# Ten of the twelve column blocks of the mixer's input projections as seven block products, their results kept in DRAM

## The chip, the core and the metric

One core of a Trainium2 chip. Five engines work side by side, each in its own program order: PE (matrix products; its weight loads are listed as PEld), DVE and ACT (element-wise work), POOL, and SP, which only issues transfers. They wait for each other through semaphores. Working memory is SBUF (128 partitions); matrix products land in PSUM, in banks of 128 x 512 fp32. The metric is the device time of one execution in microseconds.

## What is computed

One layer of a hybrid decoder for 512 tokens of width 2048, in fp32:

```python
def token_mixer(h, ...):
    proj = h @ w_in
    gq, gk, gv, gg, ga, dq, dk, dv = [...]
    log_a = jax.nn.log_sigmoid(ga @ w_alpha_up + b_alpha) / GLA_TAU
    o_a = gla_chunked(gq, gk, gv, log_a)
    o_a = rmsnorm(o_a, gla_norm) * jax.nn.silu(gg)
    o_b = rmsnorm(diff_attention(dq, dk, dv, lam), diff_norm) * (1.0 - lambda_init)
    return jnp.concatenate([o_a, o_b], axis=-1) @ w_o

x = x + rmsnorm(token_mixer(rmsnorm(x, attn_pre_norm), ...), attn_post_norm)
x = x + rmsnorm(conv_ffn(rmsnorm(x, ffn_pre_norm), ...), ffn_post_norm)
```

There are four heads of gated linear attention (GLA; queries and keys 128 wide, values 256) and four of differential attention (two pairs of queries and keys of 128, values 256). `conv_ffn` is a gated MLP of width 5632 with a short convolution; the change does not touch it.

## The kernel before

**Products.** Every fp32 operand is kept as a high and a low half, and a product is three matmuls: high by high, high by low, low by high. The normed tokens stand transposed in `ah` and `al`, 16 slices of 128 of the 2048 inputs. Weights come in granules of 512 KB (128 x 1024) into `raw` tiles, four of them; for each granule ACT copies the high half (L136) and DVE subtracts it for the low half (L137), both into `ring`, which has three slots for each half. A slot is free again when PE has used it.

**Column blocks.** The mixer's input weights are twelve blocks of 512 columns: GV (two), GQ with GK (256 columns each, two), DV (two), DQ with DK (four) and the gate GG (two). `proj_n` (L190 to L192) makes rows of tokens: tokens are the stationary operand, 512 weight columns move, eight granules of two slices. `proj_t` (L172 to L174) makes transposed results for queries and keys: 128 weight columns are stationary, 512 tokens move, four granules for 256 columns. Both take 192 matmuls of 512 columns for a block. Results stay in SBUF: `gv`, `dv`, the q and k tiles, `oa` (GLA's output, gated in place by `gate`) and `dst` (the differential heads' output, already transposed).

**Heads.** The forget gate (`forget_gate`, L396 to L408), the GLA heads and the differential heads are generators in a list `fill`. After each granule `step` moves the first one on, 1.7 steps per granule at first and 1.0 from the first differential head on. A differential head goes through four blocks of 128 queries. For each there are two score products (L508), the softmax (max, exponential, sums; L510 to L524, where L523 scales and L524 subtracts the second map from the first), the transposes (L531), the product with the values (L539) and the transposes of the result (L551). Within a block each step waits for the one before.

**What sets the order.** A scheduler puts each engine's instructions in order when the kernel is built; on the chip each engine follows that order. Only the first half of the first block and the passage to the FFN are written out by hand.

**The FFN's up projection** already has the form that the change brings to the mixer: with the tokens in two halves, the inputs in two and the columns in two, a product of 2 x 2 blocks is made from seven products in place of eight (class `Unit`, segments `x0`, `z0`, `y0`, `z1`, `x1`, `y1`, `y2`). The token sums for it are made once. The weight sums are made partly by DVE and partly by transfers that add to what lies in SBUF (`more`, issued by POOL). Its matmuls (L928 to L930) have 256 columns, and its halves lie in `ring` at the offsets `APART = (16, 112)`, while the mixer's are at `LEVEL = (0, 0)`.

Of the kernel before, what the change touches and what calls it, by code (L numbers as in the profile page):

```python
# [9 lines left out]
F32 = mybir.dt.float32  # L10
# [7 lines left out]
P = 128  # L18
# [17 lines left out]
def hybrid_layer(ctx: ExitStack, tc: tile.TileContext, x, attn_pre_norm, w_in, w_alpha_up, b_alpha,  # L36
# [69 lines left out]
    LEVEL, APART = (0, 0), (16, 112)  # L106
# [99 lines left out]
    mixer = ExitStack()  # L206
    mx1 = mixer.enter_context(tc.tile_pool(name="mx1", bufs=1))
    mx = mixer.enter_context(tc.tile_pool(name="mx", bufs=6))

    def big8(name):  # L210
        return mx.tile([P, 2048], F32, name=name, tag="big8", bufs=6)

    def qk_tile(name):
        return mx.tile([P, S], F32, name=name, tag="qk", bufs=6)

    def tmp(name, shape=(P, S)):
        return mx.tile(list(shape), F32, name=name, tag="tmp")


    def first_half(c):  # L220
        gb = big8("gb")
        jb = mx.tile([P, 1024], F32, name="jb", tag="jb", bufs=1)
        xts = [big8("xt") for _ in range(NT)]
        w3 = mx.tile([P, 2, GR], F32R, name="w3", tag="big8", bufs=6)
# [84 lines left out]
    gv = [big8("gv").rearrange("p (t e) -> p t e", t=NT) for _ in range(2)]  # L309

    def gv_out(c):
        return lambda t, b: act(gv[c][:, t, :], b, AF.Copy)

    proj_n(w_in3, C_GV, gv_out(0), first=4, banks=banks)


    dist = mx1.tile([P, S], F32, name="dist")
    nc.gpsimd.iota(dist, [[-1, S]], base=S - P, channel_multiplier=1, allow_small_or_imprecise_dtypes=True)
    nc.gpsimd.affine_select(dist, dist, [[-1, S]], ALU.is_ge, 1e34, base=S - P, channel_multiplier=1)
    masks = mx1.tile([P, 7, 4 * 64], U8, name="masks")  # L320
    setup = big8("setup")
    for li, hs in enumerate(LEVELS):
        nb = 64 // hs
        m = setup[:, 1024 + 64 * li:1024 + 64 * (li + 1)]
# [5 lines left out]
    keep = mx1.tile([P, S], F32, name="keep")  # L330
    nc.vector.memset(keep, 1.0)
    nc.vector.memset(keep.rearrange("p (c x) -> p c x", c=4)[:, :, 0:1], 0.0)
    gnb = mx1.tile([P, GDV], F32, name="gnb")
    bcast_row(gnb, gla_norm[0])
    dnb = mx1.tile([P, DDV], F32, name="dnb")
    bcast_row(dnb, diff_norm[0])
    ts(dnb, dnb, 1.0 - LAMBDA_INIT, None, ALU.mult)

    lam = few.tile([P, 1], F32, name="lam")
    lt = setup[:, 0:512].rearrange("p (a d) -> p a d", a=4)  # L340
    for i, v in enumerate((lambda_q1, lambda_k1, lambda_q2, lambda_k2)):
        bcast_row(lt[:, i, :], v[0])
    lp = setup[:, 512:768].rearrange("p (a d) -> p a d", a=2)
# [10 lines left out]
    rows = setup[:NF, 1536:2048].rearrange("p (a d) -> p a d", a=4)  # L354
    ba = setup[:4, 768:896]
# [12 lines left out]


    bcs = big8("bcum")  # L370
    bcum = [bcs[:, h * S:(h + 1) * S] for h in range(GH)]

    def forget_gate():
        gar = tmp("gar").rearrange("p (k r) -> p k r", r=RANK)[:, :KT, :]
        dma(gar, w_in3[:, :, C_GA:C_GA + RANK])
        gas = mx.tile([P, KT, 80], F32R, name="gas", tag="big8", bufs=6)
        nc.vector.memset(gas.bitcast(F32), 0.0)
        split(gas[:, :, 0:RANK], gas[:, :, 64:64 + RANK], gar)
        wup = mx.tile([80, GH * GDK], F32, name="wup", tag="tmp")
        nc.vector.memset(wup, 0.0)  # L380
        dma(wup[0:RANK, :], w_alpha_up[0])
        dma(wup[64:64 + RANK, :], w_alpha_up[0])
        yield
# [5 lines left out]
        gaT = mx.tile([80, S], F32, name="gaT", tag="tmp")  # L389
# [3 lines left out]
        a = big8("za")  # L393
        for h in range(GH):
            zb = bank()
            mm(zb, wup[:, h * P:(h + 1) * P], gaT, start=True, stop=True)  # L396
            bcol = cols[:, h:h + 1]
            act(a[:, h * S:(h + 1) * S], zb, AF.Abs, bias=bcol)
            ts(bcum[h], zb, bcol, 0.0, ALU.add, ALU.min)
            if h % 2:  # L400
                yield
# [946 lines left out]
```

## Time and profile before

| | us |
|---|---|
| median of three runs | 2148.33 |
| their range | 2145.24 to 2149.51 |
| the profiled execution | 2149.06 |
| its span | 2147.3 |
| of it: start, 0 to 68.09 | 68.09 |
| input blocks and heads, 68.09 to 640 | 571.91 |
| end of the last gate block, transposes, 640 to 665 | 25.00 |
| output projection, 665 to 797 | 132.00 |
| passage to the FFN, 797 to 934 | 137.00 |
| up projection, 934 to 1685 | 751.00 |
| down projection and end, 1685 to 2147 | 462 |

The granted clock of the core is 0.998 over the span. Over the whole span PE is busy 2109.6 us (98%), DVE 1414.1 (66%), ACT 897.5 (42%) and POOL 199.6 (9%); these shares are averages over stages with different limits. A matmul's busy time overlaps with the next one's, so PE's pace is read from the distance between starts.

### The profile page before, as it was taken

To read this page: it belongs to the slowest core of one execution; us is meant where nothing else is said; L and a number is where in the kernel's file an instruction comes from. 1 tells how busy PE (TensorE), PEld (TensorE's weight loads), DVE (VectorE), ACT (ScalarE), POOL (GpSimd) and SP (SyncE) were. 2 spreads that over 40 slices of the span, in tenths; PEclk is the share of its full clock that TensorE was granted. 3 is DMA by queue.
4 is the path that set the end of the run, shared out by engine and by line. 5 is a ranking of instruction groups with operands and counts; after the bars stand their busy time and mean duration, and the time that the engine had idled before them with its cause. 6 is when DMAs were issued, how large, how long until landed. Compare 5 with 4: busy or idle time off the path is not lost.

```text
span 2147.3 us, 31857 instructions
## 1 busy us (share of the span) xinstructions
PE 2109.6 (98%) x13009; PEld 1872.4 (87%) x13009; DVE 1414.1 (66%) x1725; ACT 897.5 (42%) x1162; POOL 199.6 (9%) x242
## 2 busy tenths in 40 slices
PE   7999999999999999999999999999999999999998
PEld 6878888888888888899999999999999877788786
DVE  5345554443444237588778777787877867888887
ACT  4233332333343224345444444554454654443433
POOL 1000000000000001010111101111011111110100
PEclk9999999999999999999999999999999999999999
DMA  6322222223224335356775767758577787676653
GB/s 214 100 74 79 79 70 79 79 79 85 78 84 167 98 128 186 118 116 145 167 182 133 165 166 170 170 131 198 144 168 194 201 227 178 171 196 171 164 163 144
DMA packets 218471, 303.83 MB, mean 141 GB/s; under 512 B 11776, under 2 KB 155572, under 8 KB 216404
## 3 DMA queue, kind: packets, MB, share of 16 engines
q1 hardware_dynamic: 165204, 238.87, 33.4%
q0 software_dynamic: 53120, 62.92, 18.9%
q8 instruction: 102, 1.67, 0.3%
q14 instruction: 45, 0.37, 0.1%
HBM read 273.97 MB, written 27.79 MB: 141 GB/s over the span
## 4 chain that ended last, share of the span: by engine, by line
issue 51%; PE 40%; POOL 4%; DVE 2%; DMA 2%; ACT 1%; POOLq 0%; SPq 0%; DVEq 0%; ACTq 0%
PE bank L190 7%; PE bank L191 7%; PE bank L192 7%; PE bank L174 5%; PE bank L172 5%; PE bank L173 5%; POOL rt L876 2%; POOL raw L876 2%; PE bank L440 1%; PE bank L508 1%; PE bank L539 1%; PE bank L157 1%; DMA raw<-in_w_ffn_out_dram 1%; DVE ring L137 1%; DMA xt<-in_x_dram 1%
## 5 line engine op out<-in xcount | busy, mean ns | idle before, releaser
L137 DVE TENSOR_TENSOR ring<-raw,ring 128x1024 fp32r<-128x1024 f32 x305 | 371.8, 1222 | 357.1 <-ACT ring L136 350.0
L136 ACT ACTIVATE ring<-raw 128x1024 fp32r<-128x1024 f32 x305 | 322.5, 1060 | 605.1 <-PE bank L192 157.3
L930 PE MATMUL bank<-ah,ring 128*128 128x256 f32 x1280 | 353.5, 276 | 0.8 <-DVE ring L137 0.8
L928 PE MATMUL bank<-ah,ring 128*128 128x256 f32 x1280 | 353.4, 276 | 0.0
L929 PE MATMUL bank<-al,ring 128*128 128x256 f32 x1280 | 353.3, 276 | 0.0
L137 DVE TENSOR_TENSOR ring<-rt,ring 128x1024 fp32r<-128x1024 f32 x221 | 269.0, 1221 | 91.4 <-ACT ring L136 91.0
L136 ACT ACTIVATE ring<-rt 128x1024 fp32r<-128x1024 f32 x221 | 233.1, 1059 | 226.6 <-PE bank L929 144.7
L930 PEld LDWEIGHTS bank<-ah,ring 128*128 128x128 f32 x1280 | 240.3, 188 | 1.0 <-DVE ring L137 1.0
L928 PEld LDWEIGHTS bank<-ah,ring 128*128 128x128 f32 x1280 | 240.3, 188 | 0.3 <-ACT ring L136 0.2
L929 PEld LDWEIGHTS bank<-al,ring 128*128 128x128 f32 x1280 | 240.3, 188 | 0.1
L190 PE MATMUL bank<-ring,ah 128*128 128x512 f32 x600 | 236.8, 398 | 0.4 <-ACT ah L149 0.4
L191 PE MATMUL bank<-ring,ah 128*128 128x512 f32 x600 | 235.6, 393 | 0.0
L192 PE MATMUL bank<-ring,al 128*128 128x512 f32 x600 | 234.9, 393 | 0.0
L172 PE MATMUL bank<-ah,ring 128*128 128x512 f32 (+1 forms) x512 | 195.8, 383 | 1.9 <-ACT ring L136 1.9
L174 PE MATMUL bank<-ah,ring 128*128 128x512 f32 (+1 forms) x512 | 194.2, 380 | 0.1
L173 PE MATMUL bank<-al,ring 128*128 128x512 f32 (+1 forms) x512 | 194.2, 379 | 0.0
L1031 PE MATMUL bank<-ring,ah 128*128 128x512 f32 x424 | 166.3, 392 | 4.7 <-DVE ring L137 4.7
L1032 PE MATMUL bank<-ring,al 128*128 128x512 f32 x424 | 165.2, 390 | 0.0
L1030 PE MATMUL bank<-ring,ah 128*128 128x512 f32 x424 | 158.4, 391 | 1.4 <-ACT ring L136 1.0
L192 PEld LDWEIGHTS bank<-ring,al 128*128 128x128 f32 x600 | 113.0, 188 | 24.2 <-DVE al L150 0.3
L191 PEld LDWEIGHTS bank<-ring,ah 128*128 128x128 f32 x600 | 113.3, 189 | 23.7 <-DVE ring L137 0.5
L190 PEld LDWEIGHTS bank<-ring,ah 128*128 128x128 f32 x600 | 113.1, 189 | 23.7 <-ACT ah L149 0.8
(263 smaller groups left out, 4062.8 us busy)
## 6 DMA issues: line engine op xcount, KB each, us to landing
raw<-in_w_in_dram SPq DMA_DIRECT2D x96, 512.0 KB, 3.7
raw<-in_w_ffn_in_dram SPq DMA_DIRECT2D x96, 512.0 KB, 5.2
raw<-in_w_ffn_out_dram SPq DMA_DIRECT2D x48, 512.0 KB, 6.5
rt<-in_w_ffn_in_dram SPq DMA_DIRECT2D x40, 512.0 KB, 5.7
rt<-in_w_ffn_in_dram POOLq DMA_DIRECT2D x40, 512.0 KB, 6.1
raw<-in_w_ffn_in_dram POOLq DMA_DIRECT2D x40, 512.0 KB, 7.1
raw<-in_w_o_dram SPq DMA_DIRECT2D x32, 512.0 KB, 3.7
rt<-in_w_ffn_out_dram SPq DMA_DIRECT2D x20, 512.0 KB, 8.2
```

The lines of the kernel that those rows point to most:

```text
L136: act(hi, raw, AF.Copy)
L137: tt(lo, raw, hi.bitcast(F32), ALU.subtract)
L172: mm(o, wh, ah[:, t0:t1, kk, :], start=st, stop=False)
L173: mm(o, wh, al[:, t0:t1, kk, :], start=False, stop=False)
L174: mm(o, wl, ah[:, t0:t1, kk, :], start=False, stop=sp)
L190: mm(banks[t], ah[:, t, s, :], w[0][:, k, :], start=st, stop=False)
L191: mm(banks[t], ah[:, t, s, :], w[1][:, k, :], start=False, stop=False)
L192: mm(banks[t], al[:, t, s, :], w[0][:, k, :], start=False, stop=sp)
L928: mm(o, wh, sh[:, :, kk, :], start=start and kk == 0 and n == 0, stop=False, **NOW)
L929: mm(o, wh, sl[:, :, kk, :], start=False, stop=False, **NOW)
L930: mm(o, wl, sh[:, :, kk, :], start=False, stop=kk == HK - 1, **NOW)
L1031: mm(b[j], sh[:, o:o + P], w[1][:, q, :], start=False, stop=False, **NOW)
```

## The change

Two of the twelve blocks stay: GV 0 by `proj_n`, and GQ and GK of heads 0 and 1 by `proj_t`. The ten others become units (`InUnit`) of seven segments. `rows_unit` (GV 1, both DV) and `gate_unit` (both GG) have the token sums as stationary and 256 weight columns as moving operand (L699 to L701 of the changed kernel; offsets `APART_N`, the two of `APART` exchanged). `pair_unit` (GQ with GK, DQ with DK) has weights stationary and 256 tokens moving (L695 to L697). The ring's slots get a stride of 1152 elements in place of 1024. `in_sums` makes the token sums s5, s2 and s3 in six tiles, and s7, which takes the place of a quarter of `ah` and `al`.

For room, results go to DRAM (`gvd`, `dvd`, `gqd`, `gkd`, `dqd`, `dkd`, `bcd`, `oad`, `dstd`, `ogd`), and each head loads what it needs into one value tile and four tiles for queries and keys. The forget gate works on four tiles, one for each head, in place of one. The scale of L523 goes from DVE to ACT, and the product of decay and key is made for the half that is used. `pace` is 1.35 at first and 0.62 in the units. At the end, `place_diff` loads and splits the differential heads' results, and `turn_gate` transposes the gated ones, around the last unit's segments.

```diff
-    LEVEL, APART = (0, 0), (16, 112)
+    LEVEL, APART, APART_N = (0, 0), (16, 112), (112, 16)
+    RS = GR + P
     place_w = [LEVEL]
...
-        return [ring[:, GR * i + p:GR * (i + 1) + p] for i, p in zip((slot[0], slot[0] + 3), place_w[0])]
+        return [ring[:, RS * i + p:RS * i + p + GR] for i, p in zip((slot[0], slot[0] + 3), place_w[0])]
...
+    def in_sums():
+        for i in range(2):
...
+            q = flat("q")
+            tt(q, a21[0], a22[0], ALU.subtract)
+            tt(q, q, a21[1], ALU.add)
+            tt(q, q, a22[1], ALU.subtract)
+            split(sums["s5"][0][:, i], sums["s5"][1][:, i], q)
...
+            s7raw.append(r)
+            yield
...
-        a = big8("za")
+        za, bt = [], []
         for h in range(GH):
             zb = bank()
             mm(zb, wup[:, h * P:(h + 1) * P], gaT, start=True, stop=True)
             bcol = cols[:, h:h + 1]
-            act(a[:, h * S:(h + 1) * S], zb, AF.Abs, bias=bcol)
-            ts(bcum[h], zb, bcol, 0.0, ALU.add, ALU.min)
+            za.append(qk_tile("za"))
+            bt.append(tmp("bt"))
+            act(za[h], zb, AF.Abs, bias=bcol)
+            ts(bt[h], zb, bcol, 0.0, ALU.add, ALU.min)
             if h % 2:
                 yield
-        act(a, a, AF.Exp, scale=-1.0)
-        act(a, a, AF.Ln, bias=1.0)
+        for m in za:
+            act(m, m, AF.Exp, scale=-1.0)
+        for m in za:
+            act(m, m, AF.Ln, bias=1.0)
         yield
-        for h in range(GH):
-            m = a[:, h * S:(h + 1) * S]
-            tt(m, bcum[h], m, ALU.subtract)
-            nc.vector.tensor_tensor_scan(bcum[h], keep, m, 0.0, ALU.mult, ALU.add)
+        for h, m in enumerate(za):
+            tt(m, bt[h], m, ALU.subtract)
+            nc.vector.tensor_tensor_scan(bt[h], keep, m, 0.0, ALU.mult, ALU.add)
+            dma(bcd[h], bt[h])
...
+    def gla_head(h):
+        q, k, b = (qk_tile(n) for n in ("gq", "gk", "gb"))
+        dma(q, gqd[h // 2][:, h % 2, :])
+        dma(k, gkd[h // 2][:, h % 2, :])
+        dma(b, bcd[h])
+        e0 = (h % 2) * GDV
+        room = mx.tile([P, NT * GDV + 256], F32, name="gvt", tag="v", bufs=1)
...
+        dma(vt, gvd[h // 2][:, :, e0:e0 + GDV])
+        yield
...
+            o = row_tile("o")
+            stt(o, po[:, :GDV], r, gnb, ALU.mult, ALU.mult)
+            dma(oad[h][:, c, :], o)
...
-            ts(ps[1][:, :nk], ps[1][:, :nk], r2, None, ALU.mult)
+            act(ps[1][:, :nk], ps[1][:, :nk], AF.Copy, scale=r2)
...
+            o = row_tile("dst")
+            act(o, ob[:, :2 * P], AF.Copy)
+            dma(dstd[h][:, :, qb * P:(qb + 1) * P], o.rearrange("p (j c) -> p j c", j=2))
...
+    class InUnit:
+        def __init__(self, turned, cols, done):
+            self.turned, self.cols, self.done = turned, cols, done
+            self.banks = {}
+
+        def block(self, i, j, g):
+            return w_in3[:, HK * i + 4 * g:HK * i + 4 * g + 4, self.cols[j]:self.cols[j] + 256]
+
...
+        def more(self, raws, i, j):
+            for g in range(2):
+                nc.gpsimd.dma_start(out=raws[g].rearrange("p (a b) -> p a b", a=4),
+                                    in_=self.block(i, j, g), accum_op=ALU.add)
+
+        def run(self, seg, op, raws):
+            first = seg in ("x0", "z0", "x1")
+            c = "x" if seg == "x1" else "z" if seg[0] == "z" else "y"
+            b = self.banks[c] = bank(psm) if first else self.banks[c]
+            sh, sl = sums[op]
+            for g in range(2):
+                place_w[0] = APART if self.turned else APART_N
+                wh, wl = granule(None, 4, raws[g])
+                for n in range(2):
+                    o = b[:, 256 * n:256 * (n + 1)]
+                    for k in range(4):
+                        kk = 4 * g + k
+                        st, sp_ = first and kk == 0 and n == 0, kk == HK - 1
+                        if self.turned:
+                            o2 = o.rearrange("p (t c) -> p t c", c=P)
+                            ch, cl = (w[:, k, n * P:(n + 1) * P] for w in (wh, wl))
+                            mm(o2, ch, sh[:, :, kk, :], start=st, stop=False, **NOW)
+                            mm(o2, ch, sl[:, :, kk, :], start=False, stop=False, **NOW)
+                            mm(o2, cl, sh[:, :, kk, :], start=False, stop=sp_, **NOW)
+                        else:
+                            mm(o, sh[:, n, kk, :], wh[:, k, :], start=st, stop=False, **NOW)
+                            mm(o, sl[:, n, kk, :], wh[:, k, :], start=False, stop=False, **NOW)
+                            mm(o, sh[:, n, kk, :], wl[:, k, :], start=False, stop=sp_, **NOW)
+                place_w[0] = LEVEL
+                step()
+
+        def x0(self):
+            self.t = self.load(0, 0)
+            self.run("x0", "a11", self.t)
+            self.more(self.t, 0, 1)
+            self.p1 = block_tile("p1")
+            act(self.p1, self.banks["y"], AF.Copy)
+
+        def z0(self):
+            self.run("z0", "s5", self.t)
+            self.u11 = block_tile("u11")
+            act(self.u11, self.banks["z"], AF.Copy)
+
+        def y0(self):
+            self.b22 = self.load(1, 1, wide)
+            for g in range(2):
+                tt(self.t[g], self.t[g], self.b22[g], ALU.add)
+            self.run("y0", "s2", self.t)
+            self.more(self.t, 1, 0)
+            self.u10 = block_tile("u10")
+            act(self.u10, self.banks["y"], AF.Copy)
+
+        def z1(self):
+            self.run("z1", "s3", self.b22)
+            self.more(self.b22, 0, 1)
+            tt(self.u10, self.banks["z"], self.u10, ALU.subtract)
+            self.done(1, 0, self.u10)
+
+        def x1(self):
+            b21 = self.load(1, 0)
+            self.run("x1", "a12", b21)
+            tt(self.p1, self.banks["x"], self.p1, ALU.add)
+            self.done(0, 0, self.p1)
+
+        def y1(self):
+            self.run("y1", "s7", self.b22)
+            tt(self.u11, self.u11, self.banks["y"], ALU.subtract)
+            self.done(1, 1, self.u11)
+
+        def y2(self):
+            self.run("y2", "a22", self.t)
+            u01 = block_tile("u01")
+            act(u01, self.banks["y"], AF.Copy)
+            self.done(0, 1, u01)
...
+    def rows_unit(col, dst):
+        def done(j, i, u):
+            dma(dst[:, 2 * i:2 * i + 2, 256 * j:256 * (j + 1)], two(u))
+
+        return InUnit(False, (col, col + 256), done)
+
+    def pair_unit(c0, c1, d0, d1):
+        def done(j, i, u):
+            dma((d0, d1)[j][:, :, 256 * i:256 * (i + 1)], two(u))
+
+        return InUnit(True, (c0, c1), done)
...
+            op, sg = tmp("op"), tmp("sg")
+            dma(two(op), oad[2 * c + j][:, 2 * i:2 * i + 2, :])
+            act(sg, u, AF.Sigmoid)
+            tt(u, u, sg, ALU.mult)
+            tt(u, u, op, ALU.mult)
+            if c == 0:
+                dma(ogd[:, 2 * i:2 * i + 2, 256 * j:256 * (j + 1)], two(u))
+            else:
+                kept_u[j, i] = u
...
+    def turn_gate(i):
+        for j in range(2):
+            u = qk_tile("ogt")
+            dma(two(u), ogd[:, 2 * i:2 * i + 2, 256 * j:256 * (j + 1)])
+            turn_block(0, j, i, u)
+            turn_block(1, j, i, kept_u.pop((j, i)))
+
+    def place_diff(i):
+        for h in range(DH):
+            u = qk_tile("dt")
+            dma(two(u), dstd[h][:, :, 256 * i:256 * (i + 1)])
+            split(*(v[:, 2 * i:2 * i + 2, 2 * h:2 * h + 2, :].rearrange("p t n c -> p n t c") for v in (ah, al)),
+                  u.rearrange("p (n t c) -> p n t c", n=2, t=2))
...
+    units = [rows_unit(C_GV + 512, gvd[1]), pair_unit(C_GQ + 256, C_GK + 256, gqd[1], gkd[1])]
+    after = {1: [lambda: gla_head(2), lambda: gla_head(3)]}
     for g in range(2):
+        units.append(rows_unit(C_DV + 512 * g, dvd[g]))
+        for h in (2 * g, 2 * g + 1):
+            after[len(units)] = [lambda h=h: diff_head(h)]
+            units.append(pair_unit(C_DQ + 256 * h, C_DK + 256 * h, dqd[h], dkd[h]))
+    units += [gate_unit(0), gate_unit(1)]
...
+    fill.extend((in_sums(), forget_gate()))
+    pace[0] = 1.35
+    proj_n(w_in3, C_GV, gv_out, first=4, banks=banks)
+    proj_t(w_in3, C_GQ, plain_out(gqd))
+    banks = [bank(psm) for _ in range(2)]
+    for g in range(KT // 4):
+        if g == 2:
+            drain()
+            pace[:] = 0.0, 0.0
+            units[0].x0()
+        mm_t(banks, g, granule(w_in3[:, 4 * g:4 * g + 4, C_GK:C_GK + 256], 4), 0, NT)
+        step()
+    for n in range(2):
+        plain_out(gkd)(n, banks[n])
+    for i, r in enumerate(s7raw):
+        split(sums["s7"][0][:, i], sums["s7"][1][:, i], r)
+    fill.extend((gla_head(0), gla_head(1)))
+    pace[:] = 0.62, 0.0
+    units[0].z0()
+    for i, u in enumerate(units):
+        u.y0()
+        u.z1()
+        if i < len(units) - 1:
+            u.x1()
+            u.y1()
+            units[i + 1].x0()
+            u.y2()
+            for f in after.get(i, ()):
+                fill.append(f())
+            units[i + 1].z0()
+        else:
+            drain()
+            place_diff(0)
+            u.x1()
+            turn_gate(0)
+            u.y1()
+            place_diff(1)
+            u.y2()
+            turn_gate(1)
```

Two places in the engines' order. The first is ACT at the forget gate (`za` is the gate's tile, `ring<-raw` a weight granule's high half). Before:

```order
L398 ACTIVATE za<-bank,cols 128x512 [waits PE_49] x2
L136 ACTIVATE ring<-raw 128x1024 [waits DMAHW5_49,DVE_49,PE_49]
L398 ACTIVATE za<-bank,cols 128x512 [waits PE_49] x2
L402 ACTIVATE za<-za 128x2048 [waits Activation_49]
L403 ACT_TABLE_LOAD
L403 ACTIVATE za<-za 128x2048 [waits Activation_49]
L136 ACTIVATE ring<-raw 128x1024 [waits DMAHW6_49,DVE_49,PE_49]
```

And now, where L452 is the absolute value, L457 the exponential and L459 the logarithm:

```order
L452 ACTIVATE za<-bank,cols 128x512
L457 ACT_TABLE_LOAD
L457 ACTIVATE za<-za 128x512
L452 ACTIVATE za<-bank,cols 128x512
L457 ACTIVATE za<-za 128x512
L459 ACT_TABLE_LOAD
L459 ACTIVATE za<-za 128x512
L457 ACT_TABLE_LOAD
L457 ACTIVATE za<-za 128x512
L459 ACT_TABLE_LOAD
L459 ACTIVATE za<-za 128x512 x2
L137 ACTIVATE ring<-raw 128x1024
```

Exponentials and logarithms of the heads now alternate; with one more load ahead of these rows there are five, and the next weight granule (of GK) comes behind all of them. On DVE the four scans likewise come ahead of that granule's low half. On PE the 48 matmuls of the first unit's x0 and 21 of GK stand between the gate's last matmul and that granule.

The second place is PE at the end of the mixer. Before, the last differential head stands among the products of a gate block (L190 to L192):

```order
L192 MATMUL bank<-ring,al 128x512
L190 MATMUL bank<-ring,ah 128x512
L531 MATMUL bank<-ident,s 128x128 x4
L551 MATMUL bank<-ident,on 128x128 x2
L191 MATMUL bank<-ring,ah 128x512
L192 MATMUL bank<-ring,al 128x512
```

Now, behind the last product of the last unit (L701), with the scores at L589, transposes at L612 and L632, values at L620 and the output projection at L191:

```order
L632 MATMUL bank<-ident,on 128x128 x2
L589 MATMUL bank<-dk,dq 128x128 x2
L612 MATMUL bank<-ident,s 128x128
L589 MATMUL bank<-dk,dq 128x256 x2
L620 MATMUL bank<-dvt,aT 128x256
L612 MATMUL bank<-ident,s 128x128 x2
L589 MATMUL bank<-dk,dq 128x384 x2
L632 MATMUL bank<-ident,on 128x128 x2
L620 MATMUL bank<-dvt,aT 128x256 x2
L612 MATMUL bank<-ident,s 128x128 x3
L589 MATMUL bank<-dk,dq 128x512 x2
L632 MATMUL bank<-ident,on 128x128 x2
```

Head 3 has moved behind the mixer's last product, and no projection matmul stands between its steps until the output projection, three matmuls further on. On SP the loads of `dt` (the heads' results, for the output projection) stand behind head 3's own loads and wait for tiles that its queries and keys hold.

More of the change, by code (lines that the diff above doesn't have):

```diff
@@ L308, in hybrid_layer @@
         banks = first_half(0)
[L309 to L319, printed above, removed]
@@ L463, in gla_head @@
                 tt(kd, kd, k, ALU.mult)
+                qb = tmp("qb")
+                act(qb, b, AF.Exp, scale=1.0 / TAU)
+                tt(qb, q, qb, ALU.mult)
             level(li, hs, *cur)
```

241 lines of the change are left out of this document (139 added, 102 removed).

## The prediction

> **What bounds the kernel now.** I read the table of stretches first, then the list of PE's waits, then the timeline inside the stretches. The columns of the first view are the length of the stretch, then PE, weight loads, DVE, ACT and POOL busy with their instructions, the granted clock, the DMA share and GB/s.
>
> ```profile
> core 0: us, PE busy (x) PEld busy (x) DVE busy (x) ACT busy (x) POOL busy (x), PEclk, DMA share, GB/s
> 68.09:640.00 571.91, 571.44 (x2667) 470.38 (x2666) 271.17 (x503) 195.85 (x345) 31.98 (x69) 1.00 0.27 80
> 665.00:797.00 132.00, 132.00 (x584) 109.30 (x583) 41.08 (x41) 37.30 (x52) 0.00 (x0) 1.00 0.39 132
> 934.00:1685.00 751.00, 748.76 (x6593) 747.71 (x6593) 581.86 (x593) 363.90 (x399) 99.36 (x78) 1.00 0.68 160
> ...
> PE bank L531 <- DVE s L524: 0.5, 1, 0.5
> ```
>
> 68 to 640 is the mixer (the first block's second half, then the other input blocks with the heads threaded in), 665 to 797 the output projection, 934 to 1685 the up projection, which already uses seven block products. In the mixer PE is busy 571.4 of 571.9 us, and the last row, the only wait longer than a tenth or two that the list of PE's waits has between 68 and 665, is half a microsecond. DVE is busy 271 of 572 us (47%). So the mixer lasts as long as its matmuls take, and every added wait on PE counts in full.
>
> A "busy" PE is not PE at its peak, so I price matmuls by the distance between starts.
>
> ```profile
> 754.67 0.39 PE L190 MATMUL bank<-ring,ah 128*128 128x512 f32 x1
> ...
> 759.43 0.39 PE L190 MATMUL bank<-ring,ah 128*128 128x512 f32 x1
> 1299.43 0.28 PE L928 MATMUL bank<-ah,ring 128*128 128x256 f32 x1
> ...
> 1303.17 0.28 PE L928 MATMUL bank<-ah,ring 128*128 128x256 f32 x1
> 869.92 0.28 PE L172 MATMUL bank<-ah,xhi 128*128 128x256 f32 x1
> ...
> 873.52 0.28 PE L172 MATMUL bank<-ah,xhi 128*128 128x256 f32 x1
> ```
>
> From 754.67 to 759.43 lie 21 matmuls of 512 columns: 0.2267 us each. In the up projection 33 matmuls of 256 columns lie between 1299.43 and 1303.17: 0.1133 each, just half. Where the weights lie in the tiles xhi and xlo, which have no offset against each other, 30 of them take 3.60 us: 0.1200 each.
>
> **The change, part by part.**
>
> *The products.* A block of 512 columns is 192 matmuls of 512 columns (64 tiles, three each): 192 × 0.2267 = 43.52 us. A unit is seven segments of two granules with 24 matmuls of 256 columns each: 336 × 0.1133 = 38.08 us. It saves 5.44 us, ten units **54.4 us**. The heads' matmuls stay as they are.
>
> *The sums, DVE and ACT.* The first two rows are the weight splits (DVE 1.22 us, ACT 1.06 us for a granule), the third a 512-wide operation of DVE.
>
> ```profile
> L137 DVE TENSOR_TENSOR ring<-raw,ring 128x1024 fp32r<-128x1024 f32 x305 | 371.8, 1222 | 357.1 <-ACT ring L136 350.0
> L136 ACT ACTIVATE ring<-raw 128x1024 fp32r<-128x1024 f32 x305 | 322.5, 1060 | 605.1 <-PE bank L192 157.3
> L407 DVE TENSOR_TENSOR za<-bcum,za 128x512 f32<-128x512 f32 x4 | 2.5, 687 | 3.8 <-ACT za L403 3.8
> ```
>
> A unit gives DVE 14 splits (17.1 us), two weight sums (2.4) and about three result sums from PSUM (3 × 0.69 = 2.1): 21.6 us in place of a block's eight splits (9.8). About 10.5 blocks lie in the stretch 68 to 640; that is 103 us of its 271 DVE us, so 168 belong to the heads. Afterwards 168 + 216 = 384 us of DVE work lie in some 518 us, or 74%. The up projection runs at 77% (581.86 of 751) and loses 2.2 us (751.00 - 748.76) there, so I take the vector work as hidden under the matmuls. The cover is thin where a head's chain queues behind more splits than before, in 16 query blocks and 28 levels of the GLA heads. None of them losing time is one bound; the one wait before was 0.5 us, and one such in each query block would be 8, the other. I take **4**, the middle. The operand sums (s5, s2, s3, s7) are 28 operations of DVE on granule-sized tiles, 28 × 1.22 = 34 us, and lie with 12 splits (15 us) under the 12 granules of the plain blocks, 12 × 24 × 0.2267 = 65 us: hidden, 0.
>
> *The forget gate.* Here the order changes. Before, one Exp and one Ln over all four heads needed one table load between them; now the heads' Exp and Ln alternate with five loads, and no weight split stands between them on ACT.
>
> ```profile
> L396 PE MATMUL bank<-gaT,wup x8: 590/592/594, 136.9 to 140.2; 80*128 80x512 f32 x8
> L398 ACT ACTIVATE za<-bank,cols 128x512 f32<-128x512 f32 x4 | 2.6, 686 | 12.5 <-PE bank L396 12.5
> L446 ACT ACTIVATE eb<-bcum 128x512 f32<-128x512 f32 x1 | 0.6, 633 | 1.5 <-DVE bcum L408 1.5
> L408 DVE TENSOR_TENSOR_SCAN bcum<-keep,za 128x512 f32<-128x512 f32 x4 | 4.7, 1210 | 0.0
> ...
> 143.61 1.28 ACT L403 ACT_TABLE_LOAD   x1
> 144.90 1.92 ACT L403 ACTIVATE za<-za 128x2048 f32<-128x2048 f32 x1
> ```
>
> Counted from the first of the four matmuls zb: ACT starts 0.9 us later and needs 4 × 0.69 + 8 × 0.63 + 5 × 1.28 = 14.2, up to 15.1. DVE then still has a subtraction and two scans, 0.69 + 2.42, to 18.2, and only behind them the low half of the next GK granule, 1.22: 19.4. PE meanwhile has the four zb (3.5 by the first row), 21 matmuls of GK (4.76) and the 48 of the segment x0 (5.44): 13.7. Queued behind the GK granule are the rest of GK and z0, which is the whole of PE's work. It stalls 19.4 - 13.7 = 5.7 us. Bounds: 3 (the last two scans overlap more than I count) and 11 (every hand-over between engines adds half a microsecond).
>
> [...]
>
> *After an idle stretch PE is slow.* At the start of the run, behind a wait, the matmuls stand further apart although the clock column says 1.00.
>
> ```profile
> 14.21 0.63 PE L190 MATMUL bank<-ring,ah 128*128 128x512 f32 x1
> 14.64 0.63 PE L191 MATMUL bank<-ring,ah 128*128 128x512 f32 x1
> ...
> 17.36 0.40 PE L192 MATMUL bank<-ring,al 128*128 128x512 f32 x1
> 17.60 0.40 PE L190 MATMUL bank<-ring,ah 128*128 128x512 f32 x1
> ```
>
> The first pair stands 0.43 apart, the last 0.24; eight matmuls from 14.21 to 17.36 took 3.15 us in place of 1.81. So a long stall costs 1.3 us more, and the gate's comes to **7.0**.
>
> [...]
>
> *The end of the mixer.* Before, head 3 ran inside the last gate block and the output projection followed without a gap. Now its query blocks stand on PE behind the last segment y2 with nothing between them, and the projection's first matmul waits for dt, which is loaded into tiles that head 3's queries and keys hold. The same chain from the trace, as scores, the subtraction that ends the block, values, and the tile's split:
>
> ```profile
> 562.01 0.61 PE L508 MATMUL bank<-dk,dq 128*128 128x128 f32 x4
> 565.06 0.35 DVE L524 SCALAR_TENSOR_TENSOR s<-s,rl 128x128 f32<-128x128 f32 x1
> ...
> 388.78 1.03 PE L508 MATMUL bank<-dk,dq 128*128 128x256 f32 x4
> 392.93 0.48 DVE L524 SCALAR_TENSOR_TENSOR s<-s,rl 128x256 f32<-128x256 f32 x1
> 398.32 1.46 PE L508 MATMUL bank<-dk,dq 128*128 128x384 f32 x4
> 402.35 1.02 PE L539 MATMUL bank<-dv,aT 128*128 128x256 f32 x4
> 403.17 0.62 DVE L524 SCALAR_TENSOR_TENSOR s<-s,rl 128x384 f32<-128x384 f32 x1
> 404.23 1.88 PE L508 MATMUL bank<-dk,dq 128*128 128x512 f32 x4
> ...
> L149 ACT ACTIVATE ah<-dst x8: 632/633/635, 614.6 to 630.7; 128x512 fp32r<-128x512 f32 x8
> sd0s<-s SPq DMA_DIRECT2D x8, 256.0 KB, 2.0
> sd1s<-s SPq DMA_DIRECT2D x8, 256.0 KB, 5.2
> ```
>
> Scores to the end of the subtraction: 3.4 us (562.01 to 565.41), 4.6 (388.78 to 393.41), 5.5 (398.32 to 403.79). The blocks now follow one another, since each one's scores are issued behind the transposes of the one before: 13.5. A split of 1.22 stands in the first block's DVE work and half of a table load besides (0.6). The second pair of scores with 512 columns frees the tiles after some 0.9; the load of dt takes between 2.0 and 5.2, the two rows of its size, say 3; its split 0.63 and DVE's 0.69. Sum: 20.5 us from the end of y2 to the output projection. In it lies head work of PE that before was also paid for: scores 0.61 + 1.03 + 1.46 + 1.88, and transposes and values of about 5.4 (1.02 for the second block's values), 10.4 in all. Idle: about 10. Slow matmuls after two or three such gaps add 2.5. I take **12.5**; bounds 7 (no table load, load in 2.0, one slow stretch) and 18 (load in 5.2, whole table load, three slow stretches).
>
> Sum, against the profiled execution's 2149.06 us (span 2147.3 and 1.8 around it): 2149.06 - 54.4 + 4 + 7.0 + 12.5 = 2118.2. The median of the runs shown is 2148.33, 0.7 lower: **2117.5**. With the lower bounds (10 us of losses) it is 2104, with the upper (37) 2131.
>
> **The rivals.**
>
> (a) *All hidden.* PE finds other work in both gaps, as it did before, and only some 3 us are lost: 2148.33 - 54.4 + 3 = 2097. For it speaks the 0.5 us of waits above; against it that engines run their instructions in order, and that no projection matmul stands between head 3's.
>
> (b) *The row units run at 0.1200.* Five units (GV, DV twice, GG twice) have the sums as stationary and the ring's weights as moving operand, which no row shows at 256 columns. At the spacing of xhi and xlo they lose 5 × 336 × 0.0067 = 11 us: 2129. Against it: the halves are again set 96 elements apart, with sides exchanged as the operands are.
>
> (c) *Slower: the weight feed.* z0 and y1 of each unit need a granule that POOL has added to in DRAM-to-SBUF transfers, started only when the split of the segment before is done.
>
> ```profile
> raw<-in_w_in_dram SPq DMA_DIRECT2D x96, 512.0 KB, 3.7
> raw<-in_w_ffn_in_dram POOLq DMA_DIRECT2D x40, 512.0 KB, 7.1
> rt<-in_w_ffn_out_dram POOLq DMA_DIRECT2D x20, 512.0 KB, 9.4
> ```
>
> The cover is one granule and a segment, 2.72 + 5.44 = 8.2 us, and a granule or so (2.7) by which the ring runs ahead: 10.9. With 7.1 and the two splits (2.3), 9.4, it holds, as it does in the up projection. Behind result stores and head loads on the same SP queue, with POOL's own work for the heads, it could take the 9.4 of the last row and 3.7 more for a queued load, 15.4 with the splits: 4.5 us on each of 20 segments at the worst, 2117.5 + 90. It makes the kernel slower from 1.8 us on each of the 20 (36 us in all); at a middle 2.2 us it is 2161. Against it: the DMA share of this stretch is 0.27, that of the up projection 0.68.
>
> **How the numbers follow.** My forecast 0.60, (a) 0.14, (b) 0.13, (c) 0.11, and 0.02 for losses that just balance. A difference of 0.2%, 4.3 us, is about what a measurement of this kernel can tell from no change. Faster: 0.60 + 0.14 + 0.13 = 0.87; the same 0.02; slower 0.11. The forecast's own range is 2104 to 2131; down to (a) and over (b) with some of its losses it becomes 2096 to 2137, which leaves (c) and the balance out.
>
> **What would show it.** The stretch from 68 us to the start of the up projection shorter by about 31 us; 256-column starts 0.1133 apart in both kinds of unit (b: 0.120 where the sums are stationary); one PE wait of 5 to 6 us at the GK granule, for DVE's low half, behind ACT's five loads; several waits of 2 to 4 us each for head 3's subtractions at the end, and one for ACT's dt split; up projection and later stages unchanged. The prediction is wrong if the lists of waits show granule waits in every unit (c), or neither of the two stalls (a).

## The result and the profile after

The changed kernel takes 2124.01 us (median of 4 runs, 2122.67 to 2129.36) where the kernel before takes 2148.92 beside it (4 runs): a ratio of 0.9891, 95% interval 0.9869 to 0.9912, or 24.9 us less. The forecast was 2118, range 2096 to 2137. Its profiled execution has a span of 2121.9 us.

First the table of stretches of the changed kernel, cut at its own borders (columns as in the prediction): the forget gate, the units, head 3 alone, and the start of the output projection.

```profile
67.00:123.00 56.00, 52.08 (x244) 40.52 (x243) 44.39 (x49) 31.87 (x39) 5.25 (x6) 0.97 0.52 136
123.00:599.00 476.00, 475.30 (x3866) 464.10 (x3865) 330.36 (x520) 237.81 (x375) 105.54 (x116) 1.00 0.83 188
599.00:625.00 26.00, 17.00 (x56) 11.19 (x55) 15.81 (x46) 14.20 (x37) 2.23 (x6) 0.80 0.32 96
625.00:664.50 39.50, 35.20 (x168) 28.82 (x167) 18.45 (x27) 16.52 (x27) 1.60 (x2) 0.96 0.47 153
```

In the units PE idles 0.7 us in 476. The losses lie in the three stretches beside them (3.9, 9.0 and 4.3 us without a matmul), and the clock column dips there too: 0.80 in head 3's. DVE is busy 69% in the units (330 of 476). The DMA share has risen to 0.83, from 0.27 before, and still no matmul of a unit (L695 to L701) is in the list of waits below.

The second view is the list of PE's waits from 60 to 905 us (in all, times, longest).

```profile
PE bank L612 <- DVE s L605: 9.6, 4, 4.2
PE bank L191 <- ACT ah L150: 3.9, 2, 3.5
PE bank L175 <- DVE ring L138: 2.1, 1, 2.1
PE bank L173 <- ACT ring L137: 1.9, 1, 1.9
...
```

The third is the timeline of PE at these waits, with the wait and its releaser in brackets.

```profile
119.45 0.74 PE L173 MATMUL bank<-ah,ring 128*128 128x512 f32 x1 [1.86 <-ACT ring L137]
122.67 0.80 PE L175 MATMUL bank<-ah,ring 128*128 128x512 f32 x1 [2.06 <-DVE ring L138]
...
598.88 0.28 PE L701 MATMUL bank<-ring,ah 128*128 128x256 f32 x1
604.41 0.47 PE L612 MATMUL bank<-ident,s 128*128 128x128 f32 x1 [4.23 <-DVE s L605]
604.67 1.91 PE L589 MATMUL bank<-dk,dq 128*128 128x256 f32 x4
610.16 0.44 PE L612 MATMUL bank<-ident,s 128*128 128x128 f32 x2 [2.72 <-DVE s L605]
616.57 0.55 PE L612 MATMUL bank<-ident,s 128*128 128x128 f32 x3 [1.91 <-DVE s L605]
621.72 0.55 PE L191 MATMUL bank<-ring,ah 128*128 128x512 f32 x1
```

The stall at the GK granule and head 3's chain stand where the forecast had them. The last product of the units starts at 598.88 and the output projection at 621.72, 22.8 us later. The scores of 256 columns take 1.91 us in this stretch, against the 1.03 quoted for them before.

The last view shows the distances, in an undisturbed piece of a row unit (104 distances) and of a pair unit (70), and when a group of the up projection's matmuls ran in both kernels (least, median and longest duration in ns, first and last start).

```profile
547.85 0.28 PE L699 MATMUL bank<-ring,ah 128*128 128x256 f32 x1
560.10 0.28 PE L701 MATMUL bank<-ring,in_s2h 128*128 128x256 f32 x1
435.37 0.28 PE L696 MATMUL bank<-al,ring 128*128 128x256 f32 x1
443.31 0.28 PE L697 MATMUL bank<-ah,ring 128*128 128x256 f32 x1
...
L1172 PE MATMUL bank<-ah,ring x1280: 276/276/391, 905.7 to 1674.8; 128*128 128x256 f32 x183
```

And of the kernel before:

```profile
L930 PE MATMUL bank<-ah,ring x1280: 276/276/388, 929.6 to 1700.5; 128*128 128x256 f32 x183
```

Row units stand at 12.25 / 104 = 0.1178, pair units at 7.94 / 70 = 0.1134. The up projection begins 23.9 us earlier (905.7 against 929.6), so nearly all of the gain of 24.9 was made ahead of it. This start is the measure in what follows where two profiles are compared; ratios are against the kernel before, run beside each.

### The profile page after: what moved, and what is told of

It reads as the page before. It is cut to its first block, busy times and chain, and to the rows that moved or that the text cites. A ratio compares the mean times of both kernels' runs of the same rounds, so it can differ in the third digit from the quotient of the medians.

```text
span 2121.9 us, 35562 instructions
## 1 busy us (share of the span) xinstructions
PE 2071.5 (98%) x14449; PEld 1907.2 (90%) x14449; DVE 1539.2 (73%) x1844; ACT 988.8 (47%) x1274; POOL 287.8 (14%) x306
## 4 chain that ended last, share of the span: by engine, by line
issue 54%; PE 34%; POOL 4%; DVE 3%; ACT 2%; DMA 2%; POOLq 0%; SPq 0%; DVEq 0%; ACTq 0%
PE bank L695 3%; PE bank L697 3%; PE bank L696 3%; PE bank L192 3%; PE bank L191 3%; PE bank L193 3%; PE bank L699 3%; PE bank L701 3%; PE bank L700 3%; POOL rt L1118 2%; POOL raw L1118 2%; PE bank L502 1%; DVE ring L138 1%; PE bank L589 1%; PE bank L175 1%
## 5 line engine op out<-in xcount | busy, mean ns | idle before, releaser
L137 ACT ACTIVATE ring<-raw 128x1024 fp32r<-128x1024 f32 x325 | 343.7, 1060 | 538.8 <-PE bank L1171 116.1
L138 DVE TENSOR_TENSOR ring<-raw,ring 128x1024 fp32r<-128x1024 f32 x325 | 395.6, 1221 | 230.9 <-ACT ring L137 230.7
L1172 PE MATMUL bank<-ah,ring 128*128 128x256 f32 x1280 | 353.5, 276 | 0.7 <-DVE ring L138 0.7
L1170 PE MATMUL bank<-ah,ring 128*128 128x256 f32 x1280 | 353.3, 276 | 0.0
L1273 PE MATMUL bank<-ring,ah 128*128 128x512 f32 x424 | 166.6, 393 | 4.3 <-DVE ring L138 4.2
L1274 PE MATMUL bank<-ring,al 128*128 128x512 f32 x424 | 165.2, 390 | 0.0
L1272 PE MATMUL bank<-ring,ah 128*128 128x512 f32 x424 | 159.0, 392 | 2.0 <-ACT ring L137 1.2
L191 PE MATMUL bank<-ring,ah 128*128 128x512 f32 x280 | 110.1, 399 | 4.0 <-ACT ah L150 3.9
L192 PE MATMUL bank<-ring,ah 128*128 128x512 f32 x280 | 110.5, 396 | 0.4 <-DVE ring L138 0.4
L193 PE MATMUL bank<-ring,al 128*128 128x512 f32 x280 | 108.1, 394 | 0.0
L1118 POOL DMA_DIRECT2D raw<-in_w_ffn_in_dram x40 | 51.0, 1278 | 405.4 <-DVE ring L138 402.5
L1273 PEld LDWEIGHTS bank<-ring,ah 128*128 128x128 f32 x424 | 79.6, 188 | 25.5 <-DVE ring L138 9.4
L1272 PEld LDWEIGHTS bank<-ring,ah 128*128 128x128 f32 x424 | 79.3, 188 | 21.6 <-ACT ring L137 4.9
L1118 POOL DMA_DIRECT2D rt<-in_w_ffn_in_dram x40 | 50.9, 1274 | 320.1 <-DVE ring L138 258.4
L1274 PEld LDWEIGHTS bank<-ring,al 128*128 128x128 f32 x424 | 79.6, 188 | 16.3
L695 PE MATMUL bank<-ah,ring 128*128 128x256 f32 x320 | 91.4, 285 | 0.0
```

The costliest lines, as they stand in the source:

```text
L137: act(hi, raw, AF.Copy)
L138: tt(lo, raw, hi.bitcast(F32), ALU.subtract)
L191: mm(banks[t], ah[:, t, s, :], w[0][:, k, :], start=st, stop=False)
L192: mm(banks[t], ah[:, t, s, :], w[1][:, k, :], start=False, stop=False)
L193: mm(banks[t], al[:, t, s, :], w[0][:, k, :], start=False, stop=sp)
L1118: nc.gpsimd.dma_start(out=raws[g].rearrange("p (a b) -> p a b", a=self.a), in_=self.block(0, j, g), accum_op=ALU.add)
```

## The experiments

**e1, one table load in the gate.** The logarithms' bias is read from a tile that is made from the last exponential.

```diff
+        one = small.tile([P, 2], F32, name="one", tag="ls", bufs=1)[:, 0:1]
+        ts(one, za[3][:, 0:1], 0.0, 1.0, ALU.mult, ALU.add)
         for m in za:
-            act(m, m, AF.Ln, bias=1.0)
+            act(m, m, AF.Ln, bias=one)
```

> The changed kernel, with the bias of the forget gate's logarithms read from a tile that is made from the last exponential, so that the four exponentials come before the four logarithms and one table load stands between them in place of five. Theory A (the chain on ACT with its loads sets the wait at the GK granule): four loads of 1.28 us go, the logarithms end 5.1 us earlier, the two waits of 1.9 and 2.1 us at that granule and the slow matmuls behind them go, and the time falls by 4 to 6 us, to 2118 to 2120. Rival B (the four scans and DVE's splits set it, whatever ACT does): the wait for DVE's low half stays at 2 us and the time falls by less than 2 us.

Measured: ratio 0.9891 (0.9868 to 0.9914), no different from the changed kernel's, since 5 us are at the limit of such a comparison. Its profile decides. The waits from 60 to 905 us, and the up projection:

```profile
PE bank L614 <- DVE s L607: 10.4, 4, 4.2
PE bank L191 <- ACT ah L150: 4.9, 2, 3.7
...
L1172 PE MATMUL bank<-ah,ring x1280: 276/276/287, 900.4 to 1669.2; 128*128 128x256 f32 x183
```

And the same segment of the pair units, first and last start, in the changed kernel and in e1:

```profile
L695 PE MATMUL bank<-in_s5h,ring x80: 276/276/467, 180.6 to 461.4; 128*128 128x256 f32 x80
L697 PE MATMUL bank<-in_s5h,ring x80: 276/276/467, 174.1 to 454.8; 128*128 128x256 f32 x80
```

Both waits at the GK granule are gone, those of the end stand, and the up projection starts 5.3 us earlier (900.4 against 905.7). In the units the gain is larger, 6.5 to 6.6 us; 1.3 of it is lost again at the end, where the two waits sum to 15.3 us against 13.5. Theory A holds for the wait: ACT's chain with its five loads set it.

**e2 and e3, a faster pace of the heads**, alone and with e1's edit.

```diff
-    pace[:] = 0.62, 0.0
+    pace[:] = 0.75, 0.0
```

> The changed kernel with 0.75 steps of the heads per granule in place of 0.62, nothing else; head 3 then lies among the matmuls of the last two units. Theory A (head 3 alone on PE behind the last product is what the end of the mixer costs): the three waits for head 3's subtractions (4.2, 2.7 and 1.9 us), the later wait of 3.5 us for ACT's split of its results and the slow matmuls between go, and the time falls by 13 to 18 us, to 2106 to 2111. Rival B (the way through DRAM sets it: the results are stored, loaded and split before the output projection can begin): a wait of 5 us or more for ACT's split stays at the border and the time falls by less than 8 us. Rival C (the heads' faster pace takes DVE from the splits): waits for the ring's halves appear in the units, 5 us or more in sum, and eat the gain.

> Both edits together: logarithms behind the exponentials and 0.75 steps per granule. Theory A: the two gains lie at different places and add up, 17 to 24 us, to 2100 to 2107. Rival: they share a cause (one wait moved to another place), and the gain is that of the larger one alone, above 2108.

Measured: e2 0.9955 (0.9939 to 0.9971), e3 0.9915 (0.9897 to 0.9933). e2 is slower than the changed kernel. e3 is 0.4% faster than e2, which is where e1's edit shows in the times, but no faster than the changed kernel. In e3's waits head 3's subtractions are gone and others have come:

```profile
PE bank L701 <- ACT ring L137: 4.1, 2, 3.4
PE bank L701 <- ACT u L726: 4.1, 1, 4.1
PE bank L634 <- DVE on L628: 3.8, 1, 3.8
PE bank L191 <- ACT ring L137: 2.8, 1, 2.8
PE bank L703 <- DVE ring L138: 2.5, 2, 1.4
PE bank L783 <- DMA ogt<-ogd: 1.9, 1, 1.9
...
```

All lie behind 573 us, in the last unit and at its border; up to there e3 has none. e2's ACT shows what they are made of:

```profile
581.86 1.28 ACT L767 ACT_TABLE_LOAD   x1
583.16 0.63 ACT L767 ACTIVATE sg<-u 128x512 f32<-128x512 f32 x1
584.05 1.05 ACT L137 ACTIVATE ring<-raw 128x1024 fp32r<-128x1024 f32 x1
618.47 0.60 ACT L724 ACTIVATE u<-bank 128x512 f32<-128x512 f32 x1 [5.57 <-DMA ogd<-p]
```

A weight split stands behind the gate's sigmoid and its table load, between a head's exponentials, and the copy of a unit's result waits 5.57 us until a gated block has been stored to DRAM and its tile is free. So none of the theories holds as put: head 3's chain was one late thing at the end, and by these rows the last gate unit's own way through ACT, the block tiles and DRAM is as late when both run together. No run tests that way by itself.

**e4, five places for the halves of the row units**, granule by granule, each with lines of its own.

```diff
-                place_w[0] = APART if self.turned else APART_N
+                if not self.turned:
+                    mix[0] = (mix[0] + 1) % 5
+                place_w[0] = APART if self.turned else MIX[mix[0]]
...
+    MIX = [(112, 16), (0, 0), (16, 112), (64, 64), (0, 64)]
```

> The changed kernel, in which the granules of the five row units take turns between five places for the halves, (112,16), (0,0), (16,112), (64,64) and (0,64), each with matmuls on lines of its own. Theory P (the place of the moving weights against the stationary sums sets the 0.1177 us between starts in the row units): the five differ, one or more at 0.1133 and (0,0) at 0.120 or above. Rival S (it is the shape: 256 neighbouring columns of weights moving, sums stationary): all five stand at 0.117 to 0.119. The whole time stays within 6 us of 2124 in either case.

Measured: 2130.79 us in its one run, 6.8 above the changed kernel's 2124 where at most 6 was expected. Undisturbed granules, first and last of 24 matmuls, at (112, 16), then at (0, 0):

```profile
141.38 0.29 PE L702 MATMUL bank<-ring,in_s2h 128*128 128x256 f32 x1
144.08 0.28 PE L704 MATMUL bank<-ring,in_s2h 128*128 128x256 f32 x1
111.76 0.28 PE L706 MATMUL bank<-ring,ah 128*128 128x256 f32 x1
114.52 0.28 PE L708 MATMUL bank<-ring,ah 128*128 128x256 f32 x1
```

2.70 / 23 = 0.117 and 2.76 / 23 = 0.120. (16, 112) is like the first, (64, 64) and (0, 64) like the second; no granule comes to 0.1133 (the least is 0.1174). Both theories hold in part: the place is worth 0.0025 of the 0.0067 between 0.1200 and 0.1133, and the rest comes with having the sums stationary and 256 neighbouring weight columns moving. What in that form costs it stays open.

**e6 and e7, units undone**: the two DV blocks, and the four blocks of differential queries and keys, as plain products of 512 columns. By then a quarter of ah and al holds s7, so these blocks are computed from the wrong tokens; the work is that of plain blocks.

```diff
-        units.append(rows_unit(C_DV + 512 * g, dvd[g]))
+        units.append(PlainUnit(C_DV + 512 * g, dvd[g]))
```

```diff
-            units.append(pair_unit(C_DQ + 256 * h, C_DK + 256 * h, dqd[h], dkd[h]))
+            units.append(PlainPair(C_DQ + 256 * h, C_DK + 256 * h, dqd[h], dkd[h]))
```

> The changed kernel with two of its five row units (both DV blocks) as plain blocks of eight products again, results through DRAM as before. By the prediction's sum a unit saves 5.44 us: 10.9 us slower than the changed kernel. By the distances measured in the changed kernel (row units 0.1189 on the mean, 39.9 us a unit; blocks of 512 columns 0.230 where heads lie between, 44.2): 4.2 each, 8.5 us slower. Rival (the vector work that a unit adds costs as much as the products save): 0 to 4 us slower.

> The changed kernel with its four units of differential queries and keys as plain blocks of eight products again. By the prediction's sum 5.44 us each: 21.8 us slower than the changed kernel. By the measured distances (pair units 0.1155 on the mean, 38.8 us; blocks 44.2) 5.4 each: 21.4 us. Rival (the vector work eats the gain): below 12 us. With e6 it tells whether row units save less than pair units, 4.2 against 5.4 us each.

Measured: e6 0.9923 (0.9908 to 0.9938), 0.0032 or 6.9 us above the changed kernel; e7 0.9992 (0.9983 to 1.0002), 0.0101 or 21.7 us above. The profiles are sharper. The start of the last unit's second segment in the changed kernel, in e6 and in e7:

```profile
554.21 0.28 PE L699 MATMUL bank<-ring,in_s5h 128*128 128x256 f32 x1
```

```profile
562.72 0.28 PE L699 MATMUL bank<-ring,in_s5h 128*128 128x256 f32 x1
```

```profile
575.77 0.28 PE L699 MATMUL bank<-ring,in_s5h 128*128 128x256 f32 x1
```

The same segment of the first unit starts some 0.2 us later in e6 and e7 than in the changed kernel, so two row units save 8.51 - 0.2 = 8.3 us or 4.1 each, and four pair units 21.56 - 0.2 = 21.3 or 5.3 each. That is the sum by the measured distances, and it refutes the rival: vector work eats nothing of note there. The gate units, GV 1 and GQ with GK were not undone.

**e5, without head 3.**

```diff
-            after[len(units)] = [lambda h=h: diff_head(h)]
+            if h < 3:
+                after[len(units)] = [lambda h=h: diff_head(h)]
...
-            dma(two(u), dstd[h][:, :, 256 * i:256 * (i + 1)])
+            dma(two(u), dstd[min(h, 2)][:, :, 256 * i:256 * (i + 1)])
```

> The changed kernel without the fourth differential head: its four query blocks are not computed, and the output projection reads the third head's result in its place. Its matmuls, about 13 us of PE, go in any case. Theory A (head 3's serial chain on a PE with nothing else is the cost of the end): the output projection follows the last product within 3 us, the waits of 10 us for its subtractions go and so does that of 3.5 to 3.9 us for ACT's split, and the time is 26 to 32 us less than that of the changed kernel. Rival B (storing, loading and splitting the results sets the border): only the 13 us of its matmuls and a few more go, 12 to 18 us, and waits of 6 us or more for ACT's split or for a load stay at the border.

Measured: 0.9779 (0.9763 to 0.9795), 0.0112 or 24 us below the changed kernel. One wait is left at the border, and the up projection starts 25.7 us earlier:

```profile
PE bank L191 <- ACT ring L137: 4.4, 1, 4.4
...
L1172 PE MATMUL bank<-al,ring x1280: 276/276/284, 880.0 to 1650.5; 128*128 128x256 f32 x183
```

Some 13 us of it are head 3's matmuls by the estimate made before the run; the other 12 or so are then idle time and slow matmuls of its chain. The time lies 2 us short of theory A's range and 6 above rival B's: no load of results holds the border, though a weight split does for 4.4 us.

**e8, pace 1.0** with e1's edit, to end the heads well ahead of the last unit.

```diff
-    pace[:] = 0.62, 0.0
+    pace[:] = 1.0, 0.0
```

> e3's kernel with 1.0 steps of the heads per granule in place of 0.75, so that all heads end about half a unit earlier. Theory A2 (in e3 head 3 still met the last unit, and the two share ACT, the temporary tiles and SP's queue; further ahead they no longer meet): the waits of some 20 us in e3's last unit shrink to below 10, and the time falls to 0.980 to 0.986 of the kernel before. Rival B2 (the last unit's own way, gate values through DRAM and their tiles, sets it): the waits stay above 15 us and the ratio at 0.989 to 0.993. Rival C (DVE can't follow the faster pace): waits for ring halves earlier in the units, above 5 us.

Measured: 0.9882 (0.9864 to 0.9899). Its waits:

```profile
PE bank L591 <- DMA dk<-dkd: 7.3, 4, 2.7
PE bank L701 <- ACT u L717: 5.5, 1, 5.5
PE bank L614 <- DVE s L607: 2.7, 1, 2.7
...
```

The waits from the last unit on shrink to about 10 us, but the units now wait 7.3 us for keys to come back from DRAM. The total is close to B2's, by a reason that none of the theories had.

**e9, dt in another pool**: the loads that the prediction had waiting for head 3's tiles.

```diff
-            u = qk_tile("dt")
-            dma(two(u), dstd[h][:, :, 256 * i:256 * (i + 1)])
+            for n in range(2):
+                u = quarter("dt")
+                dma(u, dstd[h][:, n, 256 * i:256 * (i + 1)])
```

> The changed kernel with the loads of dt for the output projection in the pool of quarter tiles, which is free by then, in place of the four tiles that head 3's queries and keys hold; nothing else. Theory A3 (what keeps the output projection behind head 3 is that pool): its first matmuls move ahead of part of head 3's chain, the gap between the last product and the projection's start falls from 22.8 us to below 5, but most of head 3's blocks then still follow one another further on with little between them: 6 to 11 us faster than the changed kernel, ratio 0.984 to 0.987. Rival (the chain alone counts, wherever it stands): the same waits for its subtractions, ratio 0.988 to 0.991.

Measured: 0.9926 (0.991 to 0.9942): slower than the changed kernel, not faster; its up projection starts at 911.5, 5.8 us later. The output projection does start earlier, but the waits are only elsewhere:

```profile
PE bank L612 <- DVE s L605: 11.0, 4, 3.5
PE bank L191 <- ACT ah L150: 4.4, 2, 4.0
PE bank L191 <- ACT ring L137: 2.3, 1, 2.3
...
```

Head 3's blocks still follow one another with little between them, now behind the projection's first granules. Theory A3 falls: the chain costs, not the pool. Why it costs more there was not tested.

**e10 and e11, pace 0.70** with e1's edit, with dt in the quarter tiles and without.

```diff
-    pace[:] = 0.62, 0.0
+    pace[:] = 0.70, 0.0
```

> Logarithms behind exponentials, dt in the quarter tiles, and 0.70 steps per granule, by which head 3's blocks lie among the last unit's segments and the projection's matmuls. Theory A: the gate's 5 us and 12 to 18 us of the end's 22.8 go: ratio 0.980 to 0.984, 2104 to 2112 beside a kernel before of 2148. Rival B2 (as in e3 and e8, a faster pace only moves the waits to the last unit): waits of 15 us or more between the last unit's second segment and the projection, ratio 0.987 or above.

> As e10_all, with dt in the queries' and keys' pool again. Theory A3: the pool holds the projection back, and the ratio is 0.003 or more above that of e10_all. Rival: the pace alone gives the gain, both are alike within 0.002.

Measured: e10 0.9808 (0.9793 to 0.9823), 2103.52 us; e11 0.9807 (0.9783 to 0.9832), 2103.59 us. Here the kernel before took 2145.23. The pool makes no difference to the time. e11's waits from 60 to 930 us, and its up projection:

```profile
PE bank L701 <- DVE u L742: 4.0, 1, 4.0
PE bank L175 <- DVE xlo L138: 0.8, 1, 0.8
...
L1172 PE MATMUL bank<-ah,ring x1280: 276/276/287, 885.1 to 1653.5; 128*128 128x256 f32 x183
```

The two other waits are of 0.4 us. Head 3 now lies between the last unit's segments, its last block among the output projection's first matmuls (the projection starts at 607.42, the block's transposes at 609.97), and its waits have gone without new ones but for 4 us. The up projection starts 15.3 us earlier than in e1 (885.1 against 900.4), 20.6 earlier than in the changed kernel. This version beats both kernels.

## Why the prediction was right, and where its sum was off

The direction, the places of the losses and the range held; the time fell by 24.9 us where the sum had 30.8. Step by step:

- **The products** were put at 54.4 us, 5.44 for each unit. e6 and e7 give 4.1 for a row unit and 5.3 for a pair unit: 5 × 4.1 + 5 × 5.3 = 47, if the units that were not undone save as much. This is the mis-sized term, 7.4 us too much, which is more than the whole miss. The step that failed is the one that took 0.1133 us for all units. The row units stand at 0.1178; rival (b), with 0.1200 and 11 us, was two thirds right.
- **The steady units** were put at 4 us; PE idled 0.7 us there. The 77% of the up projection was the right row to lean on, and half a microsecond for each query block was too much.
- **The forget gate** was put at 5.7 us of stall and 1.3 of slow matmuls. The waits were 1.86 and 2.06, 3.9 in sum, with two matmuls between them that the sum had left out. The whole of it was well sized all the same: e1 takes back 6.6 in the units, against 7.0. The chain as counted (19.4 us from the first zb to DVE's low half) ran from 103.55 to 122.62, 19.1 us. Behind each of the five loads (1.28 us) the next ACTIVATE starts 1.29 to 1.30 us after the load's start, so the count of 5 × 1.28 held.
- **The end** was put at 20.5 us from the last product to the output projection and 12.5 of loss. The gap was 22.8. By e5 head 3's chain wastes 12 us. e11 takes back 15.3 from e1, whose end costs 1.3 more than the changed kernel's, so 14.0 of the changed kernel's, and keeps a wait of 4.0: the loss was 14 or more. The wait for ACT's split of dt was foreseen, but ahead of the projection's first matmul; that matmul is not held by it, and the wait of 3.5 us stands 34 us further on, at 655.87. The reason given, that dt must wait for tiles which head 3 holds, was wrong as a cause (e9, and e10 beside e11).
- **The weight feed**, rival (c), did not come: no unit waits for its ring. The argument that the DMA share was low fell, since it rose to 0.83; the cover by the ring sufficed all the same.
- Together: 47 - 0.7 - 6.6 - 14.0 = 25.7, and 23.9 were measured at the start of the up projection. Counted another way, the end costs some 20 us: 9.0 + 4.3 without a matmul and, as an estimate, 6.8 for the clock of 0.80 and 0.96 in the same two stretches; then the sum would be 19.6. The measured value lies between, so no run says exactly what the end cost.

That the forecast came within 6 us is in part luck: 7.4 us too much for the products and 1.5 or more too little for the end were offset by 3.3 too much for the units and 0.4 for the gate.

## What to carry to other kernels

A matmul's price belonged to its form here: the same number of columns with stationary and moving operand exchanged cost 4% more (0.1178 us between starts against 0.1134), so take the distance from a row of the same orientation. Where a chain of small dependent steps is spread under large work by a pace, look at what stands behind the last large product: 0.62, 0.70, 0.75 and 1.0 steps per granule gave ratios of 0.989, 0.981, 0.992 and 0.988 (all with e1's edit). At 0.62 the chain stands alone, at 0.75 and 1.0 other late things have come in its place, and at 0.70 under 5 us of waits are left of either; a faster pace is not better by itself. A wait that the order of instructions shows can be a symptom: moving the tile it waits for moved the wait.

## What was not expected of the hardware

- Matmuls of 256 columns with sums stationary and weights moving stand at 0.1178, with weights stationary at 0.1134; the place of the halves changes the first between 0.117 and 0.120.
- The clock column shows 0.80 in the stretch of head 3's chain, with gaps of 2 to 4 us between its steps, and the scores took 1.91 in place of 1.03 us. Cut finer, the stretch shows 0.50 three times, for some 3.3 to 3.4 us each (604.3 to 607.6, 611.1 to 614.5 and 617.9 to 621.3), and 1.00 between. The three follow the gaps of 4.23, 2.72 and 1.91 us, the last two with a delay of 0.9 and 1.3 us after PE has started again (610.16 and 616.57). No run shows what decides when the column falls. At the start of the kernel before, a like slow pace of matmuls (0.43 us between starts, 0.24 from 17.36 us on) stood beside a column of 1.00. Three of the pieces:

```profile
604.40:607.40 3.00, 2.99 (x7) 1.95 (x7) 1.59 (x5) 0.53 (x2) 0.00 (x0) 0.50 0.18 66
610.20:611.00 0.80, 0.80 (x4) 0.62 (x5) 0.00 (x0) 0.36 (x1) 0.00 (x0) 1.00 0.00 0
618.00:621.00 3.00, 3.00 (x7) 1.67 (x7) 2.68 (x5) 0.38 (x1) 0.00 (x0) 0.50 0.45 143
```

- Loads of the mixer's weights took 5.8 us to land, against 3.7 before, at three times the DMA share (0.83 in the units against 0.27), and no unit waited for one.

The page's row for the last point:

```profile
raw<-in_w_in_dram SPq DMA_DIRECT2D x56, 512.0 KB, 5.8
```
